# Attention of a hybrid block run wholly beside the second half's projection products, one stage for each product; output projections alone, with one split of W_out

## The chip, the core and the metric

The kernel runs on one core of a Trainium2 chip (NeuronCore). The metric is device time in microseconds (us), the median of several executions. The engines are TensorE (PE; its weight loads are PEld), VectorE (DVE), ScalarE (ACT), GpSimd (POOL) and SyncE (SP); here POOL and SP almost only issue DMA transfers.

## What is computed

One block on x (2048 tokens x 1024 channels, float32), depth 1:

```python
h = rmsnorm(x, norm_g)
q, k, v, z_att, gb, gc, u, z_conv, g_att, g_conv = split(h @ w_in)   # 6144 columns
att = chunked_rel_attention(q, k, v, rel_bias)     # 8 heads of 64; own 64-chunk and 8 before it
y_att  = (att * silu(z_att)) @ w_att_out
vconv  = causal_depthwise_conv(gc * u, conv_w, conv_b)               # width 3
y_conv = (gb * vconv * silu(z_conv)) @ w_conv_out
m = sigmoid(g_att) * y_att + sigmoid(g_conv) * y_conv
out = rmsnorm(x + m @ w_out, final_norm_g)
```

## The kernel before

**Numbers.** Every float32 operand of a matmul is split into a high part (an ACT cast) and a low part (a DVE subtraction), and a product is three matmuls: high x high, high x low, low x high (`passes`, L132 to L137). One product is 12 matmuls of 128x128 weights by 512 columns: four contraction tiles, three passes.

**Input projection.** The tokens go in two halves of 1024. For each half the 6144 output columns are 24 pairs of column tiles, and each pair is done by a 7-product scheme (`ORDER`, L36). `order` (L509, L510) sets which pair comes when; `names` numbers them 0 to 47, and `seq` lists the products. In the first half a pair's weights are built and split on ACT and DVE and stored; in the second half the split weights are only loaded again (`operand`, L375; 512 KB for each product, three products ahead). The results of q, k, v, z and the gates go to DRAM.

In the second half the order of pairs is 5 pairs of gates, then (before) 8 pairs of the convolution (`conv_gate()`), then the 8 pairs of q and k (4), v (2) and z (2), then 3 pairs of gates.

**Attention.** `attention` (L140) is a generator. One stage handles one unit: a chunk of 512 tokens c, a head h and a group g of 128 query rows; there are 4 x 8 x 4 = 128 units, and with the lag of `BACK` = 3 there are 131 stages. A stage issues the scores of its unit (`att_s`: 4 matmuls on PE, the bias and row maximum on DVE in L196, exp on ACT in L200, reciprocal on DVE, scaling on ACT in L202), the 5 transposes of the unit two stages back with their split (`att_t`, L210, L215, L216), and in every second stage the 12 matmuls with the values (`att_v`, L228). Chunk c = 0 has fewer key blocks and so fewer and shorter matmuls. The loads of q, k, bias, values and z go through POOL's queue (`load_qk`, `load_v`); the values have one buffer, `vv`.

Attention begins at the end of pair 28 (L774). Before, 64 of its stages are spread over the 133 products that are left (L780, L781). The other 67 are called by `pump` (L902), some 1.15 for each group of 12 matmuls of the output projections of the first half, `half_c(0)` and `half_d(0)`.

**Output projections.** For each half `half_c` (L796) does 16 items: a weight tile of w_conv_out or w_att_out is loaded (`raw_w`), split (`split_into`), multiplied with two token groups (2 products), and gated; the items of the attention side then form m and split it again (`split_pair`, mh and ml). `half_d` (L846) does m @ W_out, 16 groups of 24 matmuls, the residual and the last norm. W_out is loaded and split by `out_weights` (L826), once for each half (16 pieces each time).

**What sets the order.** Up to pair 25 the order on PE, DVE and ACT is the order of the code. From there on (`manual.close()`, L784, 785) a scheduler sets the order of the instructions on each engine from the code's dependencies; each engine then runs its queue strictly in that order. SP and POOL are ordered by the scheduler throughout.

**Buffers in question.** 56 slots of 2 KB (`tt`), 10 tiles `e` for evictions and raw weights, 4 weight tiles `wr`, 3 PSUM banks for products, one PSUM buffer each for scores, transposes and values, 5 gate tiles `gp`, which open when the convolution's buffers close (L786 to L788).

Of the kernel before, what the change touches and what calls it, by code (L numbers as in the profile page):

```python
# [10 lines left out]
F32R = mybir.dt.float32r  # L11
# [6 lines left out]
P = 128  # L18
# [5 lines left out]
CH = 512  # L24
NC = SEQ // CH
HEADS = 8
# [14 lines left out]
def block_kernel(ctx, tc, xb, xt, wp_in, wy, wo, bias, ng, fg, cw, cb, out):  # L41
# [467 lines left out]
    order = [[*range(G, G + 4), *conv_gate(G + 4, G + 5, G + 6, G + 7), *range(Q, Q + 8)]]  # L509
    order.append([G + 3, G + 4, *range(G, G + PLAIN), *conv_gate(), *range(Q, Q + 8), G + 5, G + 6, G + 7])  # L510
    names = [n * NPAIR + p for n in range(NH) for p in order[n]]
# [193 lines left out]
    ab = None  # L705
    at_stages = 0
    turned = None
    uv = {}

    for s, (p, i) in enumerate(seq):  # L710
# [63 lines left out]
        elif n == NPAIR + 1 + PLAIN and i == 3:  # L774
            first.close()
            att = ExitStack()
            ab = attention(att.enter_context(tc.tile_pool(name="ab", bufs=1, side="right")))
            s0 = s
        elif ab:
            want = (s - s0) * 64 / (len(seq) - s0)  # L780
            while at_stages < min(want, 64):  # L781
                next(ab)
                at_stages += 1
        if n == NPAIR + 1 and i == 3:  # L784
            manual.close()
        if n == NPAIR + 2 + PLAIN + 8 and i == 1:  # L786
            conv_stack.close()
            gp = pool("gp", 5)  # L788
# [3 lines left out]
    while later:  # L792
        tick()


    def half_c(hf, mids, made, pump, before):  # L796

# [5 lines left out]
        for n_, (i, d) in enumerate(ITEMS_C):  # L803
# [8 lines left out]
            for n, c in enumerate(cs):  # L812
# [6 lines left out]
                else:  # L819
                    nc.vector.tensor_add(t, t, partial.pop((d, c)))  # L820
                    m[d, c] = split_pair("m", t)
                pump()
                before(i, d, n)
# [21 lines left out]

    def half_d(hf, m, pump, prepare, at):  # L846

# [14 lines left out]
        for n, (b, h) in enumerate(items):  # L862
# [5 lines left out]
            for k in range(KT):  # L868
                while (k, h) not in wout:
                    next(prepare)  # L870
                (mh, ml), (wh, wl) = m[k, c], wout[k, h]
# [3 lines left out]
                nc.tensor.matmul(ps, lhsT=ml[:, gs], rhs=wh, start=False, stop=(k == KT - 1))  # L875
                if k == 3:
                    pump()
            y = ys[b][h]
# [6 lines left out]
            if h:  # L885
                r = rsqrt_mean(acc, 1)
                for q, y in enumerate(ys.pop(b)):
                    nc.vector.scalar_tensor_tensor(y, y, r[:, 0:1], fg_sb[q], op0=ALU.mult, op1=ALU.mult)
                    defer(0, lambda q=q, y=y, b=b: nc.sync.dma_start(out[8 * hf + b, :, q * CH:(q + 1) * CH], y))
            pump()  # L890
            if (b, h) == (3, 1):
                for k in range(KT):
                    del m[k, 2 * hf]
        while later:
            tick()
        wout.clear()

    total = NC * HEADS * 4 + BACK

    state = [0, at_stages]  # L900

    def pump():  # L902
        state[0] += 1
        want = min(total, 64 + state[0] * (total - 64) / 58)
        while state[1] < want:
            next(ab, None)
            state[1] += 1

    def ring_or_slots(n):
        if 4 <= n < 8:  # L910
            w = wtile("wo")
            return tuple(w[:, s].rearrange("p k c -> p (k c)") for s in range(2))
        return slot("woh"), slot("wol")

    prep = out_weights(ring_or_slots)

    def first_four(i, d, n):
        if i == 0 and d >= 4 and n:
            next(prep)

    m = half_c(0, mids, made, pump, first_four)
    nxt = {}

# [7 lines left out]

    half_d(0, m, pump, prep, next_half)
    m.clear()
    for _ in ab:
        pass
    att.close()
    op = pool("op", 24, side="right")
    prep = out_weights(lambda n: tuple(op.tile([P, CH], F32R, tag="wo", name="wo") for s in range(2)) if n < 12 else (slot("woh"), slot("wol")))

    def every_other(i, d, n):  # L940
        if n:
            next(prep, None)

    m = half_c(1, nxt["mids"], nxt["made"], lambda: None, every_other)
    half_d(1, m, lambda: None, prep, lambda n: None)


# [49 lines left out]
```

## Time and profile before

| what | value |
|---|---|
| median of 3 runs | 1577.24 us (1573.85 to 1580.59) |
| the profiled execution: own time / span | 1571.1 / 1569.3 us |
| granted TensorE clock, mean | 0.99 |
| busy: PE / DVE / ACT / POOL | 97% / 67% / 43% / 10% |
| DMA | 393.65 MB, mean 251 GB/s |

How to read it: PE's busy share is the union of modelled matmul times, and matmuls are pipelined (a 512-column matmul is drawn 0.39 us long and the next starts 0.23 us later), so 97% says little of how near the engine is to its limit; its idle time, and the distance between starts, say more. The span falls into stages: first half until some 600 us, second-half products with attention to 1066.7, `half_c(0)` and `half_d(0)` with the rest of attention to 1386.4, `half_c(1)` to 1473.4, `half_d(1)` to 1560.4. A window is a stretch of the span in us.

### The profile page before, as it was taken

What the parts mean: (1) busy time and instruction counts of PE and PEld (TensorE: products, weight loads), DVE (VectorE), ACT (ScalarE), POOL (GpSimd) and SP (SyncE); (2) the same over time, 40 slices, a digit from 0 to 9 for tenths busy, and PEclk for the clock granted to TensorE, in tenths of its full rate; (3) what the DMA queues carried; (4) which work ended last, traced back from release to release, by engine and by line L of the source; (5) the groups of instructions that cost most, each with busy time, mean ns of one, the idle gap of its engine ahead of it and who ended that gap; (6) DMA issues with size and microseconds to landing.
All of it is one profiled execution on the core that took longest, in us unless ns stands there. A gap on an engine that the chain in (4) does not pass through costs nothing.

```text
span 1569.3 us, 21720 instructions
## 1 busy us (share of the span) xinstructions
PE 1522.1 (97%) x7396; PEld 1268.2 (81%) x7396; DVE 1045.3 (67%) x2094; ACT 682.6 (43%) x1266; POOL 154.9 (10%) x294
## 2 busy tenths in 40 slices
PE   9899999999998999999999999999999999999997
PEld 6677878888786787888888888888887788888886
DVE  7978779797668653666565455446678786656544
ACT  6353343443335242333344444446666676523211
POOL 0000000000000001111121012012332222000000
PEclk9999999999999999999999999999999899999999
DMA  5287898989996926787899889898967668369231
GB/s 210 79 293 298 309 338 306 371 298 311 332 338 230 318 92 215 222 266 238 295 313 314 303 281 287 270 314 274 294 200 228 203 217 273 124 220 316 67 108 68
DMA packets 161711, 393.65 MB, mean 251 GB/s; under 512 B 20160, under 2 KB 40640, under 8 KB 161600
## 3 DMA queue, kind: packets, MB, share of 16 engines
q1 hardware_dynamic: 131392, 306.25, 56.2%
q0 software_dynamic: 20992, 69.22, 14.0%
q10 hardware_dynamic: 9216, 16.78, 2.9%
q8 instruction: 59, 0.97, 0.3%
q14 instruction: 52, 0.43, 0.1%
HBM read 241.18 MB, written 150.99 MB: 250 GB/s over the span
## 4 chain that ended last, share of the span: by engine, by line
PE 62%; DVE 4%; DMA 2%; ACT 1%; issue 1%; SPq 0%; DVEq 0%; ACTq 0%
PE ps_d L137 13%; PE ps_d L135 13%; PE ps_d L136 13%; PE ps_s L190 4%; PE po L228 4%; PE ps_d L873 3%; PE ps_d L875 3%; PE ps_d L874 3%; PE ps_t L210 3%; DMA wraw<-wy 1%; ACT pr L200 1%; DMA wraw<-wo 0%; DVE ps_s L196 0%; DVE ptl L216 0%; PE vt L433 0%
## 5 line engine op out<-in xcount | busy, mean ns | idle before, releaser
L158 POOL DMA_DIRECT2D q<-q x128 | 66.6, 526 | 710.4 <-DVE wc L123 603.3
L200 ACT ACTIVATE pr<-ps_s,nmax 128x640 f32<-128x640 f32 (+4 forms) x128 | 93.3, 729 | 89.8 <-DVE nmax L196 86.2
L196 DVE CUSTOM_DVE_ANT_0 ps_s<-ps_s,bs 128x640 f32<-128x640 f32 (+4 forms) x128 | 95.4, 745 | 48.1 <-PE ps_s L190 47.5
L215 ACT CAST pth<-ps_t 128x640 fp32r<-128x640 f32 (+4 forms) x128 | 79.8, 623 | 99.9 <-PE ps_t L210 98.5
L202 ACT ACTIVATE pr<-pr,rs 128x640 f32<-128x640 f32 (+4 forms) x128 | 97.7, 763 | 24.2 <-DVE rs L201 24.2
L190 PE MATMUL ps_s<-kk,q 128*128 128x320 f32 (+1 forms) x448 | 99.5, 336 | 8.5 <-ACT pr L200 8.3
L122 ACT CAST wc<-wraw 128x512 fp32r<-128x512 f32 x120 | 72.9, 619 | 76.5 <-DMA wc<-wc 41.6
L136 PE MATMUL ps_d<-mid,wy 128*128 128x512 f32 x256 | 101.4, 396 | 0.0
L135 PE MATMUL ps_d<-mid,wy 128*128 128x512 f32 x256 | 101.2, 395 | 0.0
L137 PE MATMUL ps_d<-mid,wy 128*128 128x512 f32 x256 | 101.2, 395 | 0.0
L216 DVE TENSOR_TENSOR ptl<-ps_t,pth 128x640 fp32r<-128x640 f32 (+4 forms) x128 | 94.2, 736 | 1.1 <-ACT pth L215 0.8
L123 DVE TENSOR_TENSOR wc<-wraw,wc 128x512 fp32r<-128x512 f32 x120 | 81.1, 688 | 12.5 <-ACT wc L122 11.5
L210 PE MATMUL ps_t<-ident,pr 128*128 128x128 f32 x560 | 84.2, 276 | 1.0 <-DVE ptl L216 0.8
L228 PE MATMUL po<-pth,vv 128*128 128x256 f32 x336 | 80.1, 272 | 2.3 <-ACT pth L215 2.2
L228 PE MATMUL po<-ptl,vv 128*128 128x256 f32 x336 | 78.5, 281 | 0.0
L190 PEld LDWEIGHTS ps_s<-kk,q 128*128 128x128 f32 x448 | 67.9, 191 | 13.0 <-ACT pr L200 12.3
L210 PEld LDWEIGHTS ps_t<-ident,pr 128*128 128x128 f32 x560 | 63.3, 140 | 11.1 <-issue 3.2
L228 PEld LDWEIGHTS po<-pth,vv 128*128 128x128 f32 x336 | 64.3, 191 | 6.8 <-ACT pth L215 3.4
L228 PEld LDWEIGHTS po<-ptl,vv 128*128 128x128 f32 x336 | 64.5, 192 | 2.7
L757 DVE TENSOR_TENSOR c<-v,ps_d 128x512 f32<-128x512 f32 x45 | 30.9, 687 | 48.7 <-PE ps_d L137 46.4
L884 ACT ACTIVATE sq<-y 128x512 f32<-128x512 f32 x32 | 20.2, 631 | 92.1 <-DVE y L879 92.0
L746 DVE TENSOR_TENSOR c<-u,ps_d 128x512 f32<-128x512 f32 x45 | 30.9, 686 | 42.3 <-PE ps_d L137 38.5
(370 smaller groups left out, 4260.0 us busy)
## 6 DMA issues: line engine op xcount, KB each, us to landing
wc<-wc SPq DMA_DIRECT2D x294, 512.0 KB, 4.7
wraw<-wp_in SPq DMA_DIRECT2D x54, 512.0 KB, 6.2
q<-q POOLq DMA_DIRECT2D x128, 128.0 KB, 4.9
gl<-gate SPq DMA_DIRECT2D x64, 256.0 KB, 3.9
mid<-mid SPq DMA_DIRECT2D x64, 256.0 KB, 5.7
bs<-bias POOLq DMA_DIRECT2D x32, 320.0 KB, 7.1
gate<-c ACTq DMA_DIRECT2D x34, 256.0 KB, 4.6
v<-vst SPq DMA_DIRECT2D x64, 128.0 KB, 4.6
```

What stands on the lines that cost most here:

```text
L123: nc.vector.tensor_sub(w[:, 1], src, w[:, 0].bitcast(F32))
L135: nc.tensor.matmul(ps, lhsT=w[:, 0, k, :], rhs=rh[:, cs], start=(first and k == 0), stop=False)
L136: nc.tensor.matmul(ps, lhsT=w[:, 0, k, :], rhs=rl[:, cs], start=False, stop=False)
L137: nc.tensor.matmul(ps, lhsT=w[:, 1, k, :], rhs=rh[:, cs], start=False, stop=(last and k == len(rhs) - 1))
L190: nc.tensor.matmul(ps[:, i, :m], lhsT=q[s][:, g * P:(g + 1) * P], rhs=kk[:, k1 - n + i * m:k1 - n + (i + 1) * m], start=(s == 0), stop=(s ...
L196: nc.vector.tensor_tensor_reduce(out=view, in0=view, in1=bv, scale=-0.125, scalar=3.0e38, op0=ALU.add, op1=ALU.min, accum_out=nmax)
L200: nc.scalar.activation(out, view, AF.Exp, bias=nmax, scale=-1.0, accum_out=rs)
L202: nc.scalar.activation(pr[:, :n], pr[:, :n], AF.Identity, scale=rs)
L210: nc.tensor.transpose(out=ps[:, j * P:(j + 1) * P], in_=pr[:, j * P:(j + 1) * P], identity=ident)
L215: nc.scalar.copy(hi[:, js, qs], src)
L216: nc.vector.tensor_sub(lo[:, js, qs], src, hi[:, js, qs].bitcast(F32))
L228: nc.tensor.matmul(ps[:, (g0 + a) * P:(g0 + b) * P], lhsT=vv[:, g0 + j, :], rhs=s[:, j, a * P:b * P], start=(i == 0 and s is pt[0]), stop= ...
```

## The change

1. In the second half the pairs of q, k, v and z come before those of the convolution.
2. Attention's stages are all spread over the 133 products that follow pair 28, so about one for each product; what is left is run out after the last product, and attention's buffers are closed there.
3. `half_c` and `half_d` lose the calls of `pump`. W_out is split once, in `half_c(0)`, one piece for each item: 12 pieces into 24 buffers of a pool that opens where attention's buffers were, 4 into slots. Both halves use it; `half_c(1)` splits nothing of W_out.
4. The gate tiles open 8 pairs later, at pair 45.

```diff
-    order.append([G + 3, G + 4, *range(G, G + PLAIN), *conv_gate(), *range(Q, Q + 8), G + 5, G + 6, G + 7])
+    order.append([G + 3, G + 4, *range(G, G + PLAIN), *range(Q, Q + 8), *conv_gate(), G + 5, G + 6, G + 7])
...
+    units = NC * HEADS * 4 + BACK
...
         elif ab:
-            want = (s - s0) * 64 / (len(seq) - s0)
-            while at_stages < min(want, 64):
+            while at_stages < (s - s0) * units / (len(seq) - s0 - 1):
                 next(ab)
                 at_stages += 1
...
-        if n == NPAIR + 2 + PLAIN + 8 and i == 1:
+        if n == NPAIR + 2 + PLAIN + 16 and i == 1:
             conv_stack.close()
             gp = pool("gp", 5)
...
     while later:
         tick()
+    for _ in ab:
+        pass
+    att.close()
+    op = pool("op", 24, side="right")
...
-                pump()
                 before(i, d, n)
...
-                while (k, h) not in wout:
-                    next(prepare)
...
-                if k == 3:
-                    pump()
...
-            pump()
...
-        wout.clear()
...
-    prep = out_weights(ring_or_slots)
-
-    def first_four(i, d, n):
-        if i == 0 and d >= 4 and n:
-            next(prep)
-
-    m = half_c(0, mids, made, pump, first_four)
+    prep = out_weights(lambda n: tuple(op.tile([P, CH], F32R, tag="wo", name="wo") for s in range(2)) if n < 12 else (slot("woh"), slot("wol")))
+
+    def every_other(i, d, n):
+        if n:
+            next(prep, None)
+
+    m = half_c(0, mids, made, every_other)
...
-    half_d(0, m, pump, prep, next_half)
+    half_d(0, m, next_half)
     m.clear()
...
-    m = half_c(1, nxt["mids"], nxt["made"], lambda: None, every_other)
-    half_d(1, m, lambda: None, prep, lambda n: None)
+    m = half_c(1, nxt["mids"], nxt["made"], lambda *a: None)
+    half_d(1, m, lambda n: None)
```

What it does to the order, at three places (names as in the program; a number after a line is that line of the kernel in question).

PE at the first stages of attention, in pair 29 of the second half (t23, t60: parts of the activations of a product; ps_s: scores), as the difference of the two programs:

```order
 L136 MATMUL ps_d<-t23l,wc 128x512
 L137 MATMUL ps_d<-t23h,wc 128x512
+L190 MATMUL ps_s<-kk,q_5701 128x256
+L190 MATMUL ps_s<-kk,q_5702 128x256
 L135 MATMUL ps_d<-t60h,wc 128x512
 L136 MATMUL ps_d<-t60l,wc 128x512
```

The second stage's scores now stand one product after the first's instead of two, and so on: a stage after every 12 product matmuls where it was after every 24.

DVE in the last pair of the second half, three evictions of products (u, v, c) with what stands between them. Before:

```order
L750 TENSOR_TENSOR u<-u,ps_d 128x512
L753 TENSOR_TENSOR v<-u,ps_d 128x512
L235 TENSOR_TENSOR o<-po,ot 64x512
L196 ISA ps_s,nmax<-ps_s,bs 128x2x320
L196 ISA nmax 128x1
L216 TENSOR_TENSOR ptl<-ps_t,pth 128x5x128
L201 RECIPROCAL rs<-rs 128x1
L123 TENSOR_TENSOR wy<-wraw,wy 128x512
L757 TENSOR_TENSOR c_10004<-v,ps_d 128x512
```

With the change:

```order
L747 TENSOR_TENSOR c_11868<-u,ps_d 128x512
L235 TENSOR_TENSOR o<-po,ot 64x512
L216 TENSOR_TENSOR ptl<-ps_t,pth 128x5x128
L196 ISA ps_s,nmax<-ps_s,bs 128x2x320
L196 ISA nmax 128x1
L751 TENSOR_TENSOR u<-u,ps_d 128x512
L201 RECIPROCAL rs<-rs 128x1
L196 ISA ps_s,nmax<-ps_s,bs 128x2x320
L196 ISA nmax 128x1
L216 TENSOR_TENSOR ptl<-ps_t,pth 128x5x128
L201 RECIPROCAL rs<-rs 128x1
L754 TENSOR_TENSOR v<-u,ps_d 128x512
```

One score reduction (L196, two rows) stands between three evictions before, two now: twice the attention for a product.

ACT in `half_c(0)`, items of the attention side, at the first slots of W_out (woh). Before:

```order
L215 CAST pth<-ps_t 128x5x128
L200 ACTIVATE pr,rs<-ps_s,nmax 128x640
L834 CAST woh<-wraw 128x512
L202 ACTIVATE pr<-pr,rs 128x640
L215 CAST pth<-ps_t 128x5x128
L128 CAST mh<-gl 128x512
L122 CAST wy<-wraw 128x512 x2
L200 ACTIVATE pr,rs<-ps_s,nmax 128x640
```

With the change:

```order
L122 CAST wy<-wraw 128x512
L128 CAST mh<-gl 128x512 x3
L837 CAST woh<-wraw 128x512
L128 CAST mh<-gl 128x512 x2
L837 CAST woh<-wraw 128x512
L128 CAST mh<-gl 128x512 x2
```

Before, the exp (L200) and the scaling (L202) of attention stand in one queue with casts whose input comes straight from a DMA (woh, wy); now only the casts of the projection stand there.

## Rows read from the trace of the kernel before

**Rows 1.** Busy time by stretch: from:to in us, length, busy time of PE, PEld, DVE, ACT, POOL (instructions), granted clock, DMA share, GB/s. Products with attention to 1066.7, then `half_c(0)` and `half_d(0)` in four pieces and as a whole, then `half_c(1)` and `half_d(1)`.
```profile
616.00:760.00 144.00, 143.11 (x693) 119.51 (x692) 85.42 (x190) 52.57 (x117) 21.29 (x40) 1.00 0.80 262
800.00:900.00 100.00, 99.98 (x516) 85.29 (x515) 53.48 (x105) 43.05 (x79) 15.49 (x29) 1.00 0.93 323
950.00:1066.70 116.70, 116.70 (x626) 100.88 (x625) 57.94 (x110) 52.09 (x88) 17.91 (x34) 1.00 0.88 295
1130.00:1200.00 70.00, 66.88 (x396) 57.62 (x395) 55.21 (x108) 47.47 (x83) 21.98 (x41) 1.00 0.65 216
1200.00:1240.00 40.00, 33.08 (x171) 28.13 (x170) 28.44 (x56) 23.11 (x41) 9.66 (x18) 0.87 0.67 211
1240.00:1300.00 60.00, 59.29 (x345) 50.63 (x345) 43.95 (x109) 44.83 (x83) 12.79 (x24) 1.00 0.67 216
1300.00:1371.00 71.00, 69.74 (x416) 60.57 (x415) 48.58 (x135) 43.50 (x81) 11.83 (x22) 1.00 0.61 206
1066.70:1386.40 319.70, 307.54 (x1764) 264.88 (x1764) 227.32 (x515) 204.32 (x368) 76.41 (x143) 0.98 0.68 220
1386.40:1473.40 87.00, 87.00 (x386) 72.05 (x385) 61.18 (x106) 27.20 (x47) 0.00 (x0) 1.00 0.73 249
1473.40:1560.40 87.00, 87.00 (x385) 71.90 (x383) 37.72 (x125) 12.47 (x33) 0.00 (x0) 1.00 0.22 73
```

**Rows 2.** PE in order of time: start in us, length of the drawn instructions, engine, line, operation, count. Scores of chunk c = 0 (642.24 and 680.63) and of later chunks (1013.00 and 1071.33), a values group and what follows it (1069.48 and 1070.83).
```profile
642.24 0.42 PE L190 MATMUL ps_s<-kk,q 128*128 128x128 f32 x2
...
680.63 0.59 PE L190 MATMUL ps_s<-kk,q 128*128 128x384 f32 x2
...
1013.00 0.83 PE L190 MATMUL ps_s<-kk,q 128*128 128x320 f32 x4
...
1069.48 0.28 PE L228 MATMUL po<-pth,vv 128*128 128x256 f32 x1
...
1070.83 0.73 PE L210 MATMUL ps_t<-ident,pr 128*128 128x128 f32 x5
1071.33 0.83 PE L190 MATMUL ps_s<-kk,q 128*128 128x320 f32 x4
```

**Rows 3.** `half_c(0)` around 1200 us in order of time (start, length, engine, line, operation, in brackets the idle time before it and what ended it): SP's issues, ACT's casts and exp, PE.
```profile
1192.61 8.68 SPq L544 DMA_DIRECT2D gl<-gate  x3
...
1203.71 0.43 SPq L533 DMA_DIRECT2D wraw<-wy  x1
...
1212.34 0.62 ACT L122 CAST wy<-wraw 128x512 fp32r<-128x512 f32 x1 [2.19 <-DMA wraw<-wy]
1212.87 0.79 ACT L200 ACTIVATE pr<-ps_s,nmax 128x640 f32<-128x640 f32 x1
...
1213.80 0.86 PE L190 MATMUL ps_s<-kk,q 128*128 128x320 f32 x4 [3.33 <-ACT pr L200]
```

**Rows 4.** Who SP's queue waited for between 1190 and 1230 us: total, times, longest.
```profile
SPq L544 <- DVE ml L129: 18.4, 4, 7.1
```

**Rows 5.** Busy time by stretch, columns as in rows 1, around two waits of PE in `half_c(0)`.
```profile
1215.20:1218.60 3.40, 3.40 (x10) 2.62 (x9) 2.69 (x6) 2.69 (x6) 0.00 (x0) 0.50 0.39 127
1218.60:1232.30 13.70, 10.99 (x65) 9.40 (x63) 10.26 (x18) 7.23 (x14) 1.63 (x3) 1.00 0.50 168
1232.30:1239.10 6.80, 6.00 (x18) 5.13 (x19) 4.64 (x9) 3.56 (x7) 3.75 (x7) 0.50 0.68 248
```

**Rows 6.** DVE's and ACT's costliest groups: line, engine, operation, shapes, count, busy us, mean ns, idle time before and its releaser.
```profile
L196 DVE CUSTOM_DVE_ANT_0 ps_s<-ps_s,bs 128x640 f32<-128x640 f32 (+4 forms) x128 | 95.4, 745 | 48.1 <-PE ps_s L190 47.5
L216 DVE TENSOR_TENSOR ptl<-ps_t,pth 128x640 fp32r<-128x640 f32 (+4 forms) x128 | 94.2, 736 | 1.1 <-ACT pth L215 0.8
L753 DVE TENSOR_TENSOR v<-u,ps_d 128x512 f32<-128x512 f32 x45 | 30.9, 688 | 41.3 <-PE ps_d L137 38.9 <-DMA mid<-mid 2.0
L235 DVE TENSOR_TENSOR o<-po,ot 64x512 f32<-64x512 f32 x32 | 21.9, 683 | 25.3 <-ACT ot L234 24.9
L201 DVE RECIPROCAL rs<-rs 128x1 f32<-128x1 f32 x128 | 20.6, 161 | 26.8 <-ACT pr L200 25.9
L196 DVE DVE_READ_ACCUMULATOR2_ANT nmax<- 128x1 f32 x128 | 17.7, 138 | 0.2
L835 DVE TENSOR_TENSOR wo<-wraw,wo 128x512 fp32r<-128x512 f32 x16 | 10.9, 689 | 13.0 <-ACT wo L834 13.0
L834 ACT CAST wo<-wraw 128x512 fp32r<-128x512 f32 x16 | 9.8, 618 | 28.0 <-DMA wraw<-wo 28.0
```

**Rows 7.** DMA from 616 to 1066 us: bytes and mean rate; then issues (queue, number, KB each, median us from issue to landing).
```profile
DMA packets 50460, 128.72 MB, mean 286 GB/s; under 512 B 6430, under 2 KB 14622, under 8 KB 50427
wc<-wc SPq DMA_DIRECT2D x129, 512.0 KB, 4.8
q<-q POOLq DMA_DIRECT2D x64, 128.0 KB, 5.0
bs<-bias POOLq DMA_DIRECT2D x15, 320.0 KB, 7.7
```

**Rows 8.** Busy time by stretch of 20 us, columns as in rows 1, among the products.
```profile
800.00:820.00 20.00, 19.98 (x101) 16.68 (x100) 9.64 (x22) 7.29 (x17) 3.26 (x6) 1.00 1.03 349
1040.00:1060.00 20.00, 20.00 (x114) 17.51 (x113) 8.54 (x17) 8.61 (x15) 1.43 (x3) 1.00 1.03 380
```

**Rows 9.** The loads of the values tile vv over the whole span: us from issue to landing.
```profile
DMA to landing us min/median/max: 3.4/4.5/10.7
```

More of the change, by code (lines that the diff above doesn't have):

```diff
@@ L793, in block_kernel, with half_c @@
         tick()
-    def half_c(hf, mids, made, pump, before):
+    for _ in ab:
+        pass
+    att.close()
+    op = pool("op", 24, side="right")
+    def half_c(hf, mids, made, before):
         cs = (2 * hf, 2 * hf + 1)
@@ L844, in block_kernel, with half_d @@
     wout = {}
-    def half_d(hf, m, pump, prepare, at):
+    def half_d(hf, m, at):
         ys = {}
@@ L895, in half_d @@
             tick()
-        wout.clear()
[L898 to L913, printed above, removed]
-    prep = out_weights(ring_or_slots)
-    def first_four(i, d, n):
-        if i == 0 and d >= 4 and n:
-            next(prep)
-    m = half_c(0, mids, made, pump, first_four)
+    prep = out_weights(lambda n: tuple(op.tile([P, CH], F32R, tag="wo", name="wo") for s in range(2)) if n < 12 else (slot("woh"), slot("wol")))
[3 more added lines that the diff above has]
+    m = half_c(0, mids, made, every_other)
     nxt = {}
@@ L930, in next_half @@
                 nxt["mids"][c].append(load_mid(1, n - 10, c))
-    half_d(0, m, pump, prep, next_half)
+    half_d(0, m, next_half)
     m.clear()
[L934 to L942, printed above, removed]
-    m = half_c(1, nxt["mids"], nxt["made"], lambda: None, every_other)
-    half_d(1, m, lambda: None, prep, lambda n: None)
+    m = half_c(1, nxt["mids"], nxt["made"], lambda *a: None)
+    half_d(1, m, lambda n: None)
 def kernel(**inputs):
```

## The prediction

> **What bounds the kernel now.** Begin with the busy time by stretch [rows 1]. In the last two stages, where the output projections of the second half run without attention, PE is busy 87.00 of 87.00 us in each. In the products with attention it misses 0.89 us of 144 (616 to 760) and nothing from 950 to 1066.7. In the first half's output projections it misses 319.70 - 307.54 = 12.2 us, most of it between 1130 and 1240, and there the granted clock falls too. So PE bounds all of this part, and only one stage has slack. A busy PE is not yet a full PE, so the stage's loss is worked out from the distance between starts:
>
> - A product is 12 matmuls. `half_c(1)` is 32 products in 87.0 us: 2.72 us for each.
> - A stage of attention with full chunks: from the scores at 1013.00 to those at 1071.33 [rows 2] lie 16 products and 8 stages, 58.33 us. (58.33 - 16 x 2.72) / 8 = 1.85 us for a stage. With chunk c = 0, from 642.24 to 680.63, 12 products and 6 stages take 38.39 us: 0.96 us for a stage, since it has fewer keys.
> - `half_c(0)` and `half_d(0)` took 319.7 us. Their own work is 2 x 87.0 = 174.0. The stretch counts 1764 matmuls, 768 of them projections; the other 996, at 15 for each stage (4 scores, 5 transposes, half of 12 for the values), are 66.4 stages, at 1.85 us 122.8. Sum 296.8. So **22.9 us are lost there**, and nowhere else behind 616 us is there a loss to speak of.
>
> The reader sees one cause of it in order of time [rows 3]: SP takes 8.68 us over three loads of gate tiles, because a gate tile comes free only when DVE has made the low part of m [rows 4]; the load of a raw weight behind them is issued at 1203.71; ACT's cast of that weight waits for it until 1212.34, and the exp of attention stands behind that cast in ACT's queue; PE waits 3.33 us for the exp. After this wait and the next the granted clock is 0.50 (1.2 of 2.4 GHz) for 3.40 + 6.80 us [rows 5], which costs half of that, 5.1 us. The loss is thus a meeting of three: attention's exp, casts fed by a DMA, and DVE at 55.21 of 70 us.
>
> **The change, part by part.**
>
> *Attention leaves the output projections.* No exp, no score reduction and no transposes stand there any more. What is left has the make-up of `half_c(1)`, with 16 pieces of W_out split beside it, and of `half_d(1)`: 87.0 us each with nothing missing [rows 1]. **-22.9 us**, with 122.8 us of attention to be paid elsewhere.
>
> *The same stages stand beside products.* All 131 stages go into 133 products; 122.8 us of PE time come back there, at the price measured beside products. What is new is waits. PE's step is a product and a stage, 2.72 + 1.85 = 4.57 us (3.68 with c = 0). A stage on DVE is 0.745 + 0.138 + 0.161 + 0.736 and, every fourth or eighth stage, three operations on the result, 0.34 on average: 2.12 us; products bring one addition of 0.688 each and, in the convolution's pairs, about one operation more of that size [rows 6]. That is 3.5 of 4.57 us, 77%, as much as DVE had from 1130 to 1200. But in the second half's products no cast or reduction on ACT or DVE waits for a weight's DMA: the weights come split. So the fit is to stretches without such casts: 0.89 of 144 us (0.6%) at half the density, and from 1240 to 1371, where attention was dense, 1.97 of 131 us (1.5%) [rows 1]. The product stretch will be some 133 x 2.72 + 33 x 0.96 + 98 x 1.85 = 575 us. 0.6% of it is 3.5 us, 1.5% is 8.6 us, against 0.9 us paid there now. I take 5, nearer to the lower end since the order gives each stage a whole product to hide behind, never two stages in a row: **+4 us**. The bounds are 0 and +8.
>
> *q, k, v, z first.* Their stores now meet attention at full density while c = 0. One step there moves 512 KB of weights, 2048 KB / 7 = 293 KB of q and k stores (four evictions of each, high and low, 256 KB), and for a quarter of a head 432 KB (four q pieces, half of k, 320 KB of bias, half of v, and z and the result every second head): 1237 KB, 1.267 MB in 3.68 us, 344 GB/s for 28 products (the sizes in [rows 7], the others from the tiles' shapes). Before, the stretch moved 323 GB/s on average without a wait [rows 1], and single pieces of 20 us 349 and 380 [rows 8]. So it is at the edge: nothing lost if the DMA keeps the 349, and if it falls to the mean of the stretch, 286 GB/s [rows 7], 28 x 1.267 MB take 124 us where PE needs 103: +21 us. I take **+1 us**, since pieces at this rate cost nothing, and keep +21 as a rival.
>
> The Trainium skill (DMA: Bandwidth & Descriptors, Where 436 GB/s comes from) puts the limit of one core's HBM traffic at about 358 GB/s; by it the 28 products would take an estimated 99 us, under PE's 103. The trace had 380 in one piece, so the measurement is above the page's figure.
>
> *W_out split once.* 16 casts of 0.618 us, 16 subtractions of 0.689 us and 16 loads go. In `half_c(1)` they lay beside a PE that missed nothing, so this is worth 0 there. In `half_c(0)` their part in the loss is already in the 22.9. What it costs: 8 of the 56 slots stay taken through `half_c(1)`, which then fills all 56 at one point (16 convolution results, 16 partial sums, 16 attention results, 8 of W_out). The next slot comes free when the last convolution product is read, one product (2.72 us) at most: 0, bounded by 3.
>
> *Buffers and queues.* The pool for W_out opens on attention's buffers, so its first cast waits for the last stage; W_out is wanted only 32 products (87 us) later: 0. The gate tiles open 8 pairs later, still before the first load of them, in the last pair. SP issues the results of the first stage's loads in the last pair as before, with 4.57 us for each product instead of 3.6: 0. POOL keeps its sequence of loads; each head now has 4 steps, 18.3 us, against 29.2 among products before (half of 58.33 us) and 19.3 in the dense part (319.7 / 66.4 x 4).
>
> **Sum:** -22.9 + 4 + 1 = -17.9 us. The profiled execution took 1571.1 us (span 1569.3 and 1.8 around it), so the changed kernel would take 1553.2 in its place. That execution lies 6.1 us below the median of the runs, 1577.24. On the median: 1577.2 - 17.9 = **1559 us**.
>
> **The rivals.**
>
> *The DMA gives out while q and k are stored* (chance 0.10). For: 344 GB/s wanted over 100 us, and three kinds of traffic at once; landing times would rise from the 4.8 and 7.7 us of now [rows 7]. Against: the pieces at 349 and 380. Price up to +21 on the stretch: 1559 to 1579, half of it faster, half within the bound.
>
> *Concentrating attention loses what spreading gave* (0.07). The waits belong to attention and go with it: DVE at 77% in the convolution's 56 steps, as from 1130 to 1200, where PE missed 3.12 of 70 us (4.5%). At 4.5% over the 575 us the product stretch would lose 26 us: -22.9 + 25 = +2, 1579 us, no change. Against: those waits came through casts fed by a DMA [rows 3].
> The Trainium skill (Perfetto Trace Analysis, Optimization Strategy) says that a kernel of several regimes may gain from interleaving them; this change takes interleaving away from 174 us of projections. The trace is against it here, because projections alone miss 0.00 of 87.00 us twice.
>
> *The values come late* (0.04), the slower side. There is one buffer vv. Its load is issued when a head's last values group is done and must land before the next group, two steps later less a group: 2 x 4.57 - 1.35 (1069.48 to 1070.83 [rows 2]) = 7.8 us. Landings are 3.4, 4.5 and 10.7 us (least, median, most) [rows 9]. It decides if the usual landing passes 8.9 us: then 24 heads (c above 0) lose over 1.1 us each and eat the gain. At 9.8 us it is 48 us: 1607.
>
> That the order is not what the change says can be left out: a stage does stand after every 12 matmuls on PE, and none is left in the projections.
>
> **How the numbers follow.** The forecast has 0.79, the rivals 0.10, 0.07 and 0.04. This kernel's measurement tells about 0.5% from no change: 7.9 us, so 1569.3 and 1585.1 are the bounds. Faster: 0.79 + 0.05 (the milder half of the first rival) + 0.01 (the second with fewer waits) = 0.85. Same: 0.05 + 0.05 = 0.10. Slower: 0.04 + 0.01 = 0.05. Range: downwards no new waits (-22.9, 1554.3) and 6 us more, in case the median loses the distance that its stalls may have put between it and the profiled execution: 1548. Upwards the bounds +8 and +3 and most of the first rival: 1575.
>
> **What would show it.** After 616 us: product stretch about 575 us with PE missing under 9; then four stretches of 87 us with PE fully busy; granted clock 1.00 throughout; no wait of PE for the exp over 3 us. Wrong in the first way: PE idle or DMA share at 1.0 in the first 100 us of attention; in the second: many short waits of PE for ACT L200 all along; in the third: PE waiting at L228 for vv every 18 us.

## The result, and the profile after

| | kernel before | changed kernel |
|---|---|---|
| median (lowest to highest), 4 runs each | 1577.55 us (1573.85 to 1580.59) | **1560.12 us** (1557.36 to 1562.15) |
| ratio | | **0.9895**, 95% interval 0.9866 to 0.9923 |
| profiled execution (its span) | 1571.1 us (1569.3) | 1558.15 us (1556.4) |

The change is faster by 17.4 us on the medians and by 12.9 us between the two profiled executions. The forecast was 1559 us. The two figures of the gain are kept apart below, because the terms of the forecast can only be held against the profiled pair.

Busy time of the changed kernel by stretch, columns as in [rows 1]. The first six lines are the products with attention, then `half_c(0)`, `half_d(0)`, `half_c(1)`, `half_d(1)`:

```profile
615.00:660.00 45.00, 44.76 (x230) 37.55 (x229) 26.63 (x69) 23.67 (x58) 9.57 (x18) 1.00 0.97 338
660.00:760.00 100.00, 98.96 (x536) 83.92 (x536) 63.24 (x157) 58.85 (x132) 30.05 (x56) 1.00 0.97 329
760.00:860.00 100.00, 99.66 (x595) 88.04 (x594) 64.84 (x135) 63.58 (x112) 22.46 (x42) 1.00 0.87 282
860.00:960.00 100.00, 98.38 (x571) 85.42 (x570) 71.55 (x145) 60.55 (x103) 29.12 (x55) 1.00 0.76 245
960.00:1060.00 100.00, 99.10 (x582) 86.61 (x581) 71.60 (x143) 63.18 (x108) 29.80 (x56) 1.00 0.80 259
1060.00:1198.50 138.50, 136.78 (x795) 118.78 (x794) 88.02 (x173) 85.13 (x145) 24.64 (x46) 1.00 0.85 283
1198.50:1286.00 87.50, 87.17 (x384) 71.67 (x384) 57.75 (x92) 26.67 (x46) 1.09 (x2) 1.00 0.71 237
1286.00:1373.40 87.40, 87.40 (x387) 72.39 (x386) 38.67 (x127) 13.23 (x34) 0.00 (x0) 1.00 0.44 149
1373.40:1460.00 86.60, 86.60 (x384) 71.72 (x383) 52.79 (x91) 18.69 (x32) 0.00 (x0) 1.00 0.61 201
1460.00:1547.40 87.40, 87.40 (x387) 72.28 (x385) 37.22 (x124) 11.86 (x32) 0.00 (x0) 1.00 0.23 73
```

Read the last four lines first: all four stages of output projections now take 87 us with PE busy 348.57 of 348.90 us, and the granted clock is 1.00 in every line. Where [rows 1] had 319.70 us for the first two there are 174.9. Then the first six: PE misses 5.86 of 583.5 us. The missing time is spread thin; the most is 1.62 us of 100, from 860 to 960.

What PE waited for from 612 to 1200 us (total, times, longest):

```profile
PE ps_s L190 <- ACT pr L200: 2.8, 8, 0.6
PE po L228 <- DMA vv<-v: 0.6, 1, 0.6
PE po L228 <- DVE ptl L216: 0.6, 1, 0.6
PE ps_t L210 <- DVE ptl L216: 0.6, 1, 0.6
PE po L228 <- ACT pr L202: 0.4, 2, 0.2
```

No wait is longer than 0.6 us, against 3.33 us in one place before [rows 3]. What ACT waited for in `half_c(0)` and `half_d(0)` (1198 to 1374 us) is the most telling view of the changed kernel (of its lines, those of casts that split a weight):

```profile
ACT wo L837 <- DMA wraw<-wo: 17.9, 6, 5.8
ACT wy L122 <- PE ps_d L137: 6.2, 5, 3.9
ACT wy L122 <- DMA wraw<-wy: 6.0, 2, 4.2
ACT wo L837 <- DMA gl<-gate: 3.6, 1, 3.6
```

The same two stages before:

```profile
ACT wy L122 <- DMA wraw<-wy: 7.2, 4, 2.4
ACT wo L834 <- DMA wraw<-wo: 2.9, 1, 2.9
```

The casts still wait for their loads, 23.9 us in 8 waits for a raw weight and up to 5.8 us (before 10.1 us in 5), and PE beside them misses 0.33 us. The waits were not removed. What stood behind them in ACT's row was.

**Between the two profiles**, by the starts of the matmuls: from the first scores to the first product of W_y 450.4 us before and 582.8 after (+132.4); from there to the start of `half_c(1)` 319.6 and 174.9 (-144.7); the first half -0.7; the rest is equal. Sum -13.0.

### The profile page after: what moved, and what is told of

Same layout as the page of the kernel before. It is cut to its first block, busy times and chain, and to the rows that moved or that the text cites. A ratio compares the mean times of both kernels' runs of the same rounds, so it can differ in the third digit from the quotient of the medians.

```text
span 1556.4 us, 21620 instructions
## 1 busy us (share of the span) xinstructions
PE 1513.2 (97%) x7396; PEld 1262.6 (81%) x7396; DVE 1039.9 (67%) x2078; ACT 676.1 (43%) x1250; POOL 155.0 (10%) x294
## 4 chain that ended last, share of the span: by engine, by line
PE 76%; DVE 13%; DMA 4%; ACT 3%; issue 3%; SPq 0%; POOL 0%; ACTq 0%; DVEq 0%; POOLq 0%
PE ps_d L137 18%; PE ps_d L135 17%; PE ps_d L136 17%; PE ps_d L876 4%; PE ps_d L874 4%; PE ps_d L875 4%; PE po L228 4%; PE ps_s L190 4%; PE ps_t L210 3%; DMA wc<-wc 2%; DVE wc L123 1%; DVE ptl L216 1%; DVE ps_s L196 1%; ACT pr L200 1%; DVE cv L483 1%
## 5 line engine op out<-in xcount | busy, mean ns | idle before, releaser
L200 ACT ACTIVATE pr<-ps_s,nmax 128x640 f32<-128x640 f32 (+4 forms) x128 | 93.4, 730 | 96.7 <-DVE nmax L196 96.1
L196 DVE CUSTOM_DVE_ANT_0 ps_s<-ps_s,bs 128x640 f32<-128x640 f32 (+4 forms) x128 | 95.4, 745 | 54.0 <-PE ps_s L190 53.4
L202 ACT ACTIVATE pr<-pr,rs 128x640 f32<-128x640 f32 (+4 forms) x128 | 97.8, 764 | 27.3 <-DVE rs L201 27.2
L135 PE MATMUL ps_d<-mid,wy 128*128 128x512 f32 x256 | 99.8, 390 | 0.3 <-DVE part L820 0.3
L136 PE MATMUL ps_d<-mid,wy 128*128 128x512 f32 x256 | 99.6, 389 | 0.0
L137 PE MATMUL ps_d<-mid,wy 128*128 128x512 f32 x256 | 99.6, 389 | 0.0
L123 DVE TENSOR_TENSOR wc<-wraw,wc 128x512 fp32r<-128x512 f32 x120 | 81.1, 688 | 12.2 <-ACT wc L122 12.0
L874 PE MATMUL ps_d<-wo,mh 128*128 128x512 f32 x192 | 74.7, 389 | 0.0
L875 PE MATMUL ps_d<-wo,mh 128*128 128x512 f32 x192 | 74.7, 389 | 0.0
L876 PE MATMUL ps_d<-wo,ml 128*128 128x512 f32 x192 | 74.7, 389 | 0.0
L878 DVE SCALAR_TENSOR_TENSOR y<-ps_d,y 128x512 f32<-128x512 f32 x32 | 22.1, 692 | 76.0 <-PE ps_d L876 71.1
L210 PEld LDWEIGHTS ps_t<-ident,pr 128*128 128x128 f32 x560 | 63.2, 140 | 11.4 <-DVE ptl L216 2.1
```

Of the source, the lines that this page charges most:

```text
L135: nc.tensor.matmul(ps, lhsT=w[:, 0, k, :], rhs=rh[:, cs], start=(first and k == 0), stop=False)
L136: nc.tensor.matmul(ps, lhsT=w[:, 0, k, :], rhs=rl[:, cs], start=False, stop=False)
L137: nc.tensor.matmul(ps, lhsT=w[:, 1, k, :], rhs=rh[:, cs], start=False, stop=(last and k == len(rhs) - 1))
L196: nc.vector.tensor_tensor_reduce(out=view, in0=view, in1=bv, scale=-0.125, scalar=3.0e38, op0=ALU.add, op1=ALU.min, accum_out=nmax)
L200: nc.scalar.activation(out, view, AF.Exp, bias=nmax, scale=-1.0, accum_out=rs)
L210: nc.tensor.transpose(out=ps[:, j * P:(j + 1) * P], in_=pr[:, j * P:(j + 1) * P], identity=ident)
```

## The experiments

Twelve kernels ran on three chips; each ratio is against the kernel before on the same chip (medians there 1577.76, 1577.66 and 1578.3 us). "Stretch of products" is from the first scores to W_y's first product, "the pair" is `half_c(0)` with `half_d(0)`. The kernel before and the three experiments with its density of stages and its loads took 450 to 452 us and 319.6 to 322.6 us for them. `...` marks lines left out of a diff. Two of the expectations reckon with a loss of 24.5 us where the prediction works out 22.9.

### What part of the change acts

**The order of the pairs alone** (e1_order), at the old density of stages:

```diff
-    order.append([G + 3, G + 4, *range(G, G + PLAIN), *conv_gate(), *range(Q, Q + 8), G + 5, G + 6, G + 7])
+    order.append([G + 3, G + 4, *range(G, G + PLAIN), *range(Q, Q + 8), *conv_gate(), G + 5, G + 6, G + 7])
...
-        if n == NPAIR + 2 + PLAIN + 8 and i == 1:
+        if n == NPAIR + 2 + PLAIN + 16 and i == 1:
```

> The kernel before with only the pairs moved (q, k, v, z before the convolution, gate tiles opened 8 pairs later); 64 stages beside products and 67 in the projections, W_out split twice, as before. My theory (the loss sits where attention meets the first half's output projections, and the order of pairs is only what lets attention move): no change, 1577 +- 4 us, half_c(0) and half_d(0) together 315 to 325 us, PE missing under 3 us in the products. Rival 1 (the order of pairs itself is worth something): 1560 to 1570. Rival 2 (q and k stores beside attention are at the DMA's edge): 1582 to 1590, with PE idle in the first 100 us of attention.

Measured: 1578.39 us, ratio 1.0012 (0.9988 to 1.0037); pair 320.8 us, stretch of products 451.9. At this density the order is worth nothing by itself.

**98 of the 131 stages beside products** (e2_98), in the same order, 33 left in the pair:

```diff
-            want = (s - s0) * 64 / (len(seq) - s0)
-            while at_stages < min(want, 64):
+            want = (s - s0) * 98 / (len(seq) - s0)
+            while at_stages < min(want, 98):
...
-        want = min(total, 64 + state[0] * (total - 64) / 58)
+        want = min(total, 98 + state[0] * (total - 98) / 58)
```

> Pairs moved as in the change, but 98 stages beside products and 33 in the first half's output projections (half the dose), W_out split twice. Theory A (each stage that leaves the projections takes its share of the 24.5 us with it, about 0.35 us a stage, and meets 0.1 us a stage beside products): half the gain, 1568 to 1570 us, projections of the first half 240 to 248 us. Theory B (the loss is a meeting of DVE near 80%, late loads and the exp, and goes once there is slack): nearly the whole gain, 1559 to 1564, projections 234 to 238 us. If the gain came only with the last stage (attention closed before the projections, W_out split once): 1574 or more.

Measured: 1572.64 us, ratio 0.997 (0.9949 to 0.999), a time that neither theory had given. The pair took 243.0 us, which is in theory A's range, but the stretch of products took 524.7. With 1.85 us for each stage [rows 2] that leaves 8 us lost in the pair and 11.4 in the stretch (74.3 us over that of before, for 34 stages more): 19 of 22.9 us with half of the stages gone. The loss doesn't shrink in step with the stages. The trace shows why. Here PE where products hand over to `half_c(0)` (start, length, engine, line, operation; in brackets the idle time before it and what ended it):

```profile
1141.03 1.30 PE L210 MATMUL ps_t<-ident,pr 128*128 128x128 f32 x5 [7.94 <-DVE ptl L216]
```

and ACT before it, with the same columns:

```profile
1134.71 0.62 ACT L122 CAST wy<-wraw 128x512 fp32r<-128x512 f32 x1 [10.50 <-DMA wraw<-wy]
1135.23 0.82 ACT L202 ACTIVATE pr<-pr,rs 128x640 f32<-128x640 f32 x1
```

The cast of a raw weight stands in ACT's row ahead of attention's normalisation and waits 10.50 us for its load; PE's transposes come 7.94 us late. DVE was not crowded before it (busy time, columns as in [rows 1]):

```profile
1040.00:1124.00 84.00, 83.84 (x469) 72.69 (x468) 48.63 (x96) 48.23 (x83) 19.77 (x37) 1.00 0.87 291
```

That is 58%. So this wait came without the density of the pair before (DVE 55.21 of 70 us): one normalisation behind one cast was enough.

**W_out split for each half again** (e4_twice), the rest as in the change:

```diff
-    m = half_c(1, nxt["mids"], nxt["made"], lambda *a: None)
+    wout.clear()
+    prep = out_weights(lambda n: tuple(op.tile([P, CH], F32R, tag="wo", name="wo") for s in range(2)) if n < 12 else (slot("woh"), slot("wol")))
+    m = half_c(1, nxt["mids"], nxt["made"], every_other)
```

> The change with W_out loaded and split again for the second half. My theory (these 16 casts, subtractions and loads lay beside a PE that missed nothing): no difference from the change, 1560 +- 3 us, the last two stages 87 us each. Rival (the second split is part of the gain): 1563 to 1570, with PE idle between 1373 and 1460 us.

Measured: 1563.49 us, ratio 0.992 (0.9892 to 0.9947), which holds the change's 0.9895. The time by itself falls just into the rival's range, but `half_c(1)` and `half_d(1)` take 87.0 and 86.9 us with no idle time of PE, the pair 174.7, and the change itself took 1563.59 us on another chip (e13_again below). The second split was covered, and leaving it out is worth nothing that shows.

### What made the loss

**The raw weights' loads on POOL's queue** (e3_rawpool) instead of SP's, in the kernel before:

```diff
-        nc.sync.dma_start(r4, src)
+        nc.gpsimd.dma_start(r4, src)
...
-        nc.sync.dma_start(r, wo[k, :, h * CH:(h + 1) * CH])
+        nc.gpsimd.dma_start(r, wo[k, :, h * CH:(h + 1) * CH])
```

> The kernel before, with the loads of the raw output weights (w_conv_out, w_att_out, W_out) issued on POOL's queue instead of SP's, so that they don't stand behind gate loads that wait for a buffer. My theory of the loss (SP held by gate tiles, raw weight late, ACT's cast waits, exp behind it, PE waits, clock falls): the waits of over 2 us and the half clock go, 8 to 13 us of the 24.5: 1565 to 1570 us. Rival (DVE's and ACT's queues are just full there): the waits stay, 1575 to 1580. If attention's own loads now stand behind weights on POOL: PE waits at the values or scores for a DMA, 1577 or more.

Measured: 1573.72 us, ratio 0.9985 (0.9963 to 1.0007): no change that shows, and neither theory's time. The casts went on waiting (ACT from 1068 to 1391 us, the pair):

```profile
ACT wy L122 <- DMA wraw<-wy: 11.0, 8, 4.5
```

The pair took 322.6 us. Taking the loads out from behind SP's gate tiles did not make them early; since the waits stayed, the run can't say what they cost.

**W_y's raw blocks loaded two items ahead** (e5_ahead) instead of one:

```diff
+        raws_c = [made[0], raw_w(wy[ITEMS_C[1]])]
...
-            raw, gl = made
+            raw, gl = raws_c.pop(0), made[1]
+            if n_ + 2 < len(ITEMS_C):
+                raws_c.append(raw_w(wy[ITEMS_C[n_ + 2]]))
...
```

> The kernel before, with the raw weight of each item of half_c loaded two items ahead instead of one (the gate tiles stay one ahead), so that it is issued ahead of the gates that SP waits for. Theory (PE's long waits in the first half's output projections come from casts on ACT that wait for a raw weight, with attention's exp or transposes behind them): ACT's wait for wraw<-wy falls from 7 to 11 us to under 2, PE has no wait over 2 us there before W_out's loads begin, the stretch falls from 320 to 307-314 us, time 1565 to 1572. Rival (DVE and ACT are simply full at 79%): the stretch stays at 317 to 323 us, no change in time.

Measured: 1569.74 us, ratio 0.9949 (0.9929 to 0.9969), a time as forecast; the waits and the pair are not as forecast. Its profiled execution (1573.45 us, one of its two longest) has the chain once more. SP's issues in order of time:

```profile
1127.82 4.20 SPq L544 DMA_DIRECT2D gl<-gate  x2
1132.11 0.38 SPq L533 DMA_DIRECT2D wraw<-wy  x1
```

and ACT's operations some microseconds later:

```profile
1140.94 0.62 ACT L122 CAST wy<-wraw 128x512 fp32r<-128x512 f32 x1 [5.61 <-DMA wraw<-wy]
1141.47 0.82 ACT L202 ACTIVATE pr<-pr,rs 128x640 f32<-128x640 f32 x1
```

PE waited 5.6 us at once for the high part behind it and the pair took 321.0 us; ACT's casts of W_y waited 13.2 us in all. The time speaks for the theory, the profile says that the wait was not taken away.

**Weight loads taken out of the pair.** Two kernels like the one before, with every product and all 67 stages in place; e10_near leaves the first half's W_y out of the computation, e11_near2 its W_out too. In the first (e10_near), ACT and DVE split a tile that already lies in SBUF instead of each loaded block of W_y; in the second (e11_near2) also instead of each block of W_out:

```diff
-        return raw_w(wy[i, d]), [gate(i, d, c) for c in (2 * hf, 2 * hf + 1)]
+        return None if not hf else raw_w(wy[i, d]), [gate(i, d, c) for c in (2 * hf, 2 * hf + 1)]
...
+            if not hf:
+                raw = near((mids if i else att_mids)[0][0][0])
```
```diff
-        raw = lambda n: raw_out(n % KT, n // KT)
+        raw = lambda n: raw_out(n % KT, n // KT) if done else None
...
             r = nxt.pop(0)
+            if r is None:
+                r = near1[0].bitcast(F32)
```

> The kernel before, but in half_c(0) the 16 blocks of W_y are not loaded: ScalarE and VectorE split a tile of mid that already lies in SBUF instead, so both splits, all products and all 67 stages stay and only the splits' wait for a DMA goes (the W_y weights of the first half are left out of the computation). Theory (the loss of 22 us in half_c(0) and half_d(0) comes from the cast of a W_y block that stands in ScalarE's row and waits for its load, so that exp, VectorE and PE behind it wait): ScalarE's waits for wraw in half_c(0) go, no wait of PE for exp over 3 us stands in half_c(0), the clock stays at 1.00 there, and half_c(0)+half_d(0) takes 303 to 312 us instead of 319.6 to 322.6 (W_out's blocks are still loaded, so some of the loss can stay in half_d(0)); the time 1562 to 1571. Rival (too much VectorE and ScalarE work in too few microseconds, whatever the weights come from): 317 to 323 us there and a time of 1575 to 1579. Rival (SP's queue held by gl alone): waits for gl stay, 313 to 319 us, 1571 to 1575.

> The same as e10_near, and W_out's 16 blocks of the first half aren't loaded either: a tile of m in SBUF is split in their place (the first half leaves out both weights). Theory: no weight load is left between products and second half, so what is left of the loss goes too: half_c(0)+half_d(0) 298 to 305 us (work without a loss: 174.0 + 66.4 x 1.85 = 296.8), time 1555 to 1563, no half clock behind 616 us. Rival (concentration of VectorE and ScalarE work): as in e10_near, no change from the kernel before, 317 to 323 us and 1575 to 1579. If e10_near and e11_near2 give the same time, W_y's loads alone made the loss.

Measured: 1559.44 us, ratio **0.9885** (0.9863 to 0.9907), and 1557.07 us, ratio **0.9872** (0.985 to 0.9894). Busy time over the stretch of products and the pair, columns as in [rows 1], without W_y's loads:

```profile
616.90:1067.10 450.20, 449.30 (x2304) 382.46 (x2303) 254.93 (x525) 191.49 (x373) 70.20 (x132) 1.00 0.86 286
1067.10:1374.10 307.00, 302.71 (x1764) 260.99 (x1763) 224.78 (x508) 201.24 (x362) 76.33 (x143) 1.00 0.67 216
```

and without W_y's and W_out's:

```profile
616.60:1066.30 449.70, 449.02 (x2304) 382.46 (x2303) 254.84 (x525) 191.49 (x373) 70.22 (x132) 1.00 0.86 286
1066.30:1370.50 304.20, 301.30 (x1763) 260.41 (x1762) 224.24 (x508) 200.54 (x362) 76.33 (x143) 1.00 0.64 205
```

The pair falls from 319.6 to 307.0 and 304.3 us, as forecast; the first kernel's time is 2.6 us below the forecast. DVE has the same work in it as before (224.78 against 227.32 us), the clock is 1.00, and PE's idle time is 4.3 and 2.9 us, where it is 12.2 before, 15.7 in e1_order, 14.0 in e3_rawpool and 12.9 in e5_ahead. In those four every wait of PE over 1 us in the pair stands right behind a cast that waited for its load, but for one of 1.2 us for the values in e5_ahead. The kernel before has three; one is in [rows 3], and these are the others, the second behind a cast of W_out:

```profile
1135.73 0.62 ACT L122 CAST wy<-wraw 128x512 fp32r<-128x512 f32 x1 [2.22 <-DMA wraw<-wy]
1137.71 0.39 PE L228 MATMUL po<-pth,vv 128*128 128x256 f32 x1 [2.21 <-ACT pth L215]
1231.64 0.62 ACT L834 CAST wo<-wraw 128x512 fp32r<-128x512 f32 x1 [2.91 <-DMA wraw<-wo]
1233.10 1.44 PE L190 MATMUL ps_s<-kk,q 128*128 128x320 f32 x4 [3.51 <-ACT pr L200]
```

The longest kind of wait in e10_near, from 1066 to 1375 us (total, times, longest):

```profile
PE ps_s L190 <- ACT pr L200: 2.5, 6, 0.8
```

What held SP there from 1190 to 1230 us:

```profile
SPq L544 <- DVE ml L129: 21.4, 5, 7.1
```

This answers to [rows 4]: SP is still held for gate tiles, 21.4 us here and 18.4 there. That costs nothing to speak of once no load of W_y stands behind it. So neither the density of attention nor SP's hold by itself makes most of the loss; **the cast that waits for its load does**: of the 22.9 us the first kernel gets 12.6 back and the second 15.4, and 7.4 us stay with no weight load at all. Taking the loads away without moving a single stage gains at least as much as the whole change did: 18.9 us against 14.7 for the change on the same chip (e13_again), with intervals that overlap.

Two things go with the loads and were not run by themselves. The scheduler places the casts of W_y otherwise: before, mostly two together after every fourth exp, in e10_near one after every two or three. And tiles of `e` come free for the evictions.

### What the moved stages cost

**Twice the low part of the probabilities** (e7_dve), 0.74 us of DVE more for each stage of the change:

```diff
-            nc.vector.tensor_sub(lo[:, js, qs], src, hi[:, js, qs].bitcast(F32))
+            for _ in range(2):
+                nc.vector.tensor_sub(lo[:, js, qs], src, hi[:, js, qs].bitcast(F32))
```

> The change with the low part of the transposed probabilities computed twice on DVE: 0.74 us more for each of 128 stages, DVE in a convolution step from some 3.5 to 4.2 of 4.57 us. If the small waits beside products come from DVE's queue (with the exp and the casts behind it): 10 to 30 us more than the change, 1570 to 1590, spread over the whole product stretch. If DVE has cover enough: 0 to 4 us more.

**No low part** (e12_nolow), the same work on PE and 128 subtractions of DVE less:

```diff
-            nc.vector.tensor_sub(lo[:, js, qs], src, hi[:, js, qs].bitcast(F32))
...
-                for s in pt:
+                for s in range(2):
...
-                    ... lhsT=vv[:, g0 + j, :], rhs=s[:, j, a * P:b * P] ...
+                    ... lhsT=vv[:, g0 + j, :], rhs=pt[0][:, j, a * P:b * P] ...
```

> The change, but the low part of the transposed probabilities isn't made (VectorE has 128 subtractions of 0.74 us less, 94 us) and PE multiplies the high part twice, so PE's work is the same (the low part is left out of the computation). Theory (the 9.7 us by which the stretch of products grew beyond the stages' price is lateness in VectorE's row): the stretch from the first scores to W_y's first product 573 to 578 us instead of 582.8, the time 6 to 10 us under the change, 1550 to 1554. Rival (ScalarE's chain of exp, normalise, high part, or the loads of vv): within 2 us of the change, 1558 to 1562, stretch 581 to 584 us.

Measured: 1585.62 us, ratio 1.0043 (1.0025 to 1.006), some 25 us above the change, and 1558.05 us, ratio 0.9869 (0.9846 to 0.9893). The stretch of products of the change, columns as in [rows 1]:

```profile
615.70:1198.60 582.90, 577.05 (x3298) 499.82 (x3297) 385.89 (x815) 355.05 (x656) 145.63 (x272) 1.00 0.86 284
```

with the low part made twice:

```profile
615.20:1217.20 602.00, 587.67 (x3280) 497.02 (x3279) 459.71 (x939) 347.89 (x652) 145.95 (x272) 0.99 0.81 273
```

and without it:

```profile
617.50:1193.30 575.80, 572.86 (x3297) 501.24 (x3297) 307.66 (x686) 354.47 (x654) 145.68 (x272) 1.00 0.87 288
```

DVE busy for 66% of the stretch goes with 582.9 us, 76% with 602.0, 53% with 575.8. In the second the stretch is as forecast. Its time, forecast at 1550 to 1554 us, is 5.5 us under the change's on the same chip, where 6 to 10 were forecast: the pair gave 1.3 to 2 us back (176.9 us). Both runs change two things at once: DVE's work, and the length of the way from the transposes to the products with the values, which ends at that subtraction. They don't tell these apart.

**Some of DVE's work moved to POOL** (e9_pool), in the change, 48 operations on tiles in SBUF:

```diff
-                nc.vector.tensor_mul(o, o, zs)
+                nc.gpsimd.tensor_mul(o, o, zs)
...
-                nc.vector.tensor_sub(o.bitcast(F32R), o, zs)
+                nc.gpsimd.tensor_sub(o.bitcast(F32R), o, zs)
...
-            nc.vector.tensor_mul(v, v, t)
+            (nc.gpsimd if g > 1 else nc.vector).tensor_mul(v, v, t)
```

> The change with 48 products and subtractions of the second half that touch no PSUM moved from DVE to POOL (the convolution's two gatings, and the gating of attention's result with its low part). DVE loses some 33 us between 616 and 1199. If the small waits come from DVE's queue: 1 to 5 us less than the change, 1555 to 1559. If POOL's loads for attention now come late behind its arithmetic: more than the change, with PE waiting for values or scores by DMA.

Measured: 1572.59 us, ratio 0.996 (0.9943 to 0.9977), 12 us above the change; stretch of products 594.6 us. The costliest of the moved groups on POOL, and the same group on DVE in the change (count, busy us, mean ns, idle time before):

```profile
L237 POOL TENSOR_TENSOR o<-o,zs 128x512 f32<-128x512 f32 x16 | 21.2, 1323 | 30.4 <-DVE o L235 30.4
L237 DVE TENSOR_TENSOR o<-o,zs 128x512 f32<-128x512 f32 x16 | 11.0, 685 | 0.0
```

and PE's longest waits from 620 to 1216 us:

```profile
PE ps_t L210 <- DVE ptl L216: 5.6, 4, 2.9
PE po L228 <- DMA vv<-v: 4.6, 2, 3.6
```

POOL needs 1323 ns where DVE needs 685, so the result of a pair of heads is later; and POOL also issues attention's loads, to which the wait for vv would fit; that is not shown.

**The second half's q and k stored twice** (e8_stores), in the change, which doubles their stores in the c = 0 stretch:

```diff
...
+                if g > 1:
+                    defer(1, lambda x=x: store(again.pop(), x))
...
```

> The change with every q and k result of the second half stored a second time, into memory nobody reads: 8.4 MB more within 28 products, some 425 GB/s wanted there instead of 344. If the DMA is at its edge there at 340 to 380 GB/s: those 28 products take 115 to 128 us instead of 103, time 1572 to 1585, PE waiting for weights, scores or values by DMA. If there is spare bandwidth: 0 to 3 us more.

Measured: 1571.03 us, ratio 0.9956 (0.9937 to 0.9974), 11 us above the change and between the two forecasts; the stretch of products took 594.0 us. The beginning of attention, columns as in [rows 1]:

```profile
615.00:660.00 45.00, 44.50 (x227) 37.35 (x226) 24.46 (x64) 23.05 (x56) 9.74 (x19) 1.00 1.03 372
660.00:718.00 58.00, 52.44 (x272) 43.37 (x271) 34.70 (x88) 30.46 (x73) 16.72 (x32) 0.99 1.04 387
```

and what PE waited for from 612 to 760 us:

```profile
PE ps_d L136 <- DMA wc<-wc: 4.5, 3, 3.2
PE po L229 <- DMA vv<-v: 4.0, 4, 3.0
```

At a DMA share of 1.04 and 387 GB/s weights and values come late (PE misses 5.6 of 58 us); at 372 GB/s, in the line above, PE misses 0.5 of 45. The change itself moves 338 and 329 GB/s at a share of 0.97. The stores stand in SP's queue with the weights' loads, so bandwidth and queue are not told apart.

**The change again** (e13_again), on the chip of the last four:

> The change itself again, on the same chip as the three before it, for a narrower interval and a second profile: 1559 to 1562 us; stretch of products 582 to 584 us, half_c(0)+half_d(0) 174 to 176 us. If the profile of the change that was read until now came out low or high by the first half alone, the first scores stand elsewhere than at 615.7 us and these two stretches are as they were.

Measured: 1563.59 us, ratio 0.9906 (0.9886 to 0.9927), 1.6 us above the forecast; stretch of products 583.8 us, the pair 175.6, first scores at 616.6 us. The second profile agrees with the first to 1 us in each.

## Why the prediction was right

- **The loss of 22.9 us goes.** Measured: the pair gave up 144.7 us, 122.8 of them the stages' own price, so 21.9. The four stages of 87 us, the clock and the missing half clocks came as written. The cause, a cast that waits for its load ahead of exp, is shown for 15.4 us of it by e10_near and e11_near2, together with the place of those casts in ACT's row; e2_98 shows it with half of the stages gone. What was too narrow is "a meeting of three": the longest wait of all, 7.94 us in e2_98, came with DVE at 58%.
- **New waits beside products, +4 (0 to 8), with +1 for the stores.** The stretch grew by 132.4 us against 122.8: **+9.6**, a little above the upper bounds of 8 and 1, and the one term that was mis-sized: +5 was written (and some 575 us for the stretch without waits, which took 582.8). PE's idle time was right (5.9 us, now 5.0 more than before). The rest is no idle time: matmuls that start a little late, which a busy PE hides, as the first part of the prediction itself warned. e12_nolow bears this out: with as many matmuls PE's busy time is 572.86 us there, 577.05 in the change. It gives 7.0 us of the 9.6 to DVE's subtraction and the way through it. DVE was a little less busy than written, 72% from 860 to 1110 us, not 77%. The rate of 1.5% that was borrowed from 1240 to 1371 us counted idle time alone.
- **q, k, v, z first.** e1_order: nothing. The DMA held; in e8_stores it still did at 372 GB/s. Of the stretch 615 to 718 us PE missed 1.07 of 103 us, so +1 was fair. The landing times did rise there: 6.5 us for the weights (median), 4.8 before [rows 7].
  The prediction weighed the limit of 358 GB/s that the Trainium skill gives (DMA: Bandwidth & Descriptors, Where 436 GB/s comes from). 387 GB/s in e8_stores is above it, and the measurement decides; the same section names 425 GB/s for one transfer of 16 MB, and 387 is within that.
- **W_out split once: 0.** e4_twice agrees.
- **The sum on the profiled execution, 1553.2, was 5 us low** (1558.15), by the term above. The median came out at 1560.1 against 1559 because the median of before stood 6.4 us over its profiled execution and that of the change 2.0 (e13_again 2.9) over its own. So part of the closeness is luck: it is owed to this gap, which the range had allowed for and the sum had not. Its cause stays open. On the last chip the 11 runs of before spread over 11.5 us (1571.02 to 1582.55), the 6 each of the change and of e10_near over 4.2 and 3.6: that would fit a loss in the pair that differs from execution to execution. But e1_order's profiled execution (1578.68 us) has only 1.2 us more in the pair than that of before and its first scores 4.8 us later, in a part that no kernel here changes. The clock has a share in that: from 480 to 540 us the granted clock is 0.94 in e1_order and 1.00 before.
- **The rivals.** The DMA did not give out. The values landed as before (3.4, 4.4 and 10.8 us; [rows 9]) and PE waited for them 0.6 us. Concentration was the nearest to the truth: at DVE's 66% it costs some 7 to 10 us, and with 10 points more (e7_dve) the kernel is slower than before by 0.43%. Something like the rival's mechanism is there, without casts that wait for a load, but at the change's density it is small. The Trainium skill's advice to interleave regimes (Perfetto Trace Analysis, Optimization Strategy) is neither borne out nor refuted: e10_near interleaves as the kernel before did and, without the loads of W_y, is at least as fast as the change.

Of the kernels that do the whole work none beats the change. A kernel in which W_y's blocks are surely in SBUF before attention's last stages wasn't tried (e5_ahead, one item more, went half of the way: -7.9 us).

## What to carry to other kernels

In these traces each engine works through its row in order: an operation that is fed by a load delays everything behind it, whoever needs that (10.50 us at one cast in e2_98). Before moving work off such a stretch, price the alternative of making the load surely early; here leaving the load out gave as much as moving the work, and loading one item earlier half of it. And where an engine is called busy, measure the distance between starts in the stretch from which a rate is borrowed: idle time alone showed about half of what the denser stretch cost.

## What the runs showed of the hardware

- A transfer mix of loads and stores moved 387 GB/s for 58 us on this one core (e8_stores), and 380 was the most seen before [rows 8].
- With DVE 53, 66 and 76% busy over the stretch of products (e12_nolow, the change, e7_dve) its length was 575.8, 582.9 and 602.0 us: 7.1 us for the first 13 points and 19.1 for the next 10. The way from the transposes to the values changes in length with it; what part that has was not measured.
- An elementwise product of two 128x512 fp32 tiles took 1323 ns on POOL and 685 on DVE. The Trainium skill (GPSIMD Engine Reference, Elementwise — side-by-side cycle accounting) has a ratio of 1.96, for an addition of 2048 columns; 1.93 here agrees.
